# A planned instruction order with other prices for transfers and returns, and more PSUM banks at a phase's end and start

## The chip, the cores and the metric

The kernel runs on one core of a Trainium2 chip. TensorE (PE) multiplies matrices into the eight banks of PSUM; VectorE (DVE), ScalarE (ACT) and GpSimd (POOL) work on what lies in SBUF and PSUM; SyncE (SP) issues transfers (DMA). Each engine runs its instructions in the order in which they were written, and waits for others at semaphores. The metric is the time of one execution on the device, in microseconds (us).

## The reference, cut to what matters

It is one decoder layer in fp32, for a prompt of 1024 tokens and for eight single-token samples with a paged cache. All share their weights. A layer is a half-step feed-forward, a mixing step, and a second half-step feed-forward:

```python
h = x + 0.5 * rmsnorm(swiglu(rmsnorm(x, lp['n_ffn1_pre']), lp['ffn1_gate'], lp['ffn1_up'],
                             lp['ffn1_down']), lp['n_ffn1_post'])
u = rmsnorm(h, lp['n_mix_pre'])
proj = u @ lp['w_in']
q, k, v = jnp.split(proj[..., :3 * D_A], 3, axis=-1)
pb = proj[..., 3 * D_A:]
...
```

The columns of `proj` go to differential attention (4 heads; for the samples also over 512 cached tokens) and to an RWKV-7 recurrence (8 heads with a 64x64 state, run over the tokens). Both results are joined, multiplied by `w_out`, normalised and added to `h`; then the second feed-forward follows. The model is 1024 wide and the feed-forward 2816.

## The kernel before, in words

Activations lie transposed, 128 channels by tokens, and the tokens (prompt and samples) are cut into two halves of two chunks. The wide products keep fp32 accuracy by splitting each operand into a high and a low part and adding three products of a faster format ("split products"). Small products of the mixing are full fp32, one product each. When TensorE goes from those back to split products, this text calls it a return.

The trunk (`s_trunk`, L1031) has four phases, numbered 0 to 3 in the code, and called the first to the fourth in the prediction: the first feed-forward of half 0, that of half 1, the second feed-forward of half 0, that of half 1. Phases 0 and 3 multiply part of their blocks by a scheme with seven products in place of eight (`FAST`, `seven`); phases 1 and 2 (`WIDE`) work 512 columns wide. Each phase runs through groups of hidden blocks: gate and up products (operands `pre_X`, `pre_T` in the profile), then the down products of the group before (`trunk_xl`, and in places `trunk_dreg`). The last group's down products are called the tail here. Each tail product is evicted by VectorE into `trunk_xl`, and its squares are summed (`trunk_acc`). A stream `s_tail` then makes the norm: a product with ones (`tail_aux`; `last_aux` after phase 2), a square root on ScalarE, a reciprocal on VectorE, and a scaling of the eight blocks. During phase 1 the mixing of half 0 runs beside the wide products, during phase 2 that of half 1: projections (`proj`), four RWKV jobs a half (`job`), attention (`attn`), the output projection (`outb`), and the samples' attention over their pages (`dec_dreg`). An RWKV job brings data into another layout by a store to memory and a load back: eight times through `Md` and eight times through `Xd`.

PSUM's banks have names: m0 to m3, aux0, aux1, cb, dec. `ps()` (L246) hands a trunk product the next bank of the stream's list `banks`, which changes with the phase (L1047, L1228). Before the change phases 1, 2 and 3 open on m0 and m1 (phase 3 with aux1), and the tails of phases 1 and 2 stay on m0 and m1. `SIX` is the pair m2, m3. The four row transposes of a finished block (`rows_cb`) use the one bank cb, which a copy to `rows_X` empties.

Which engine does what, and in which order, is planned in the program. Every step of these streams is only recorded (`put`; all rows of the profile so bear one line, L325). `price` (L386) gives each a duration, and `run` (L484) then picks, again and again, the step that can start first over the five engines, within `SLACK` by its priority. For a transfer it adds up: 1.17 us from the issue to its start on the shared rings, the time on the rings, and `LAND` until it counts as seen. TensorE's steps cost more where they follow others of another kind: a return costs `MODE`. The planning is repeated `PASSES` times. Each repetition gives every step a latest start (`latest`), which orders the next one; the plan with the smallest planned end becomes the program. A price so changes the order of everything behind it, on all engines. Some steps (`either`, `choose`) also go to VectorE or to GpSimd by the plan, the subtraction that makes the low part of a weight (`wts_w`) among them.

## Time and profile before

| | |
|---|---|
| median of 3 runs | 2241.69 us (2241.63 to 2242.61) |
| the profiled execution | 2243.7 us, span 2241.9 us |
| mean granted TensorE clock | 0.994 |
| TensorE busy | 2187.3 us, 98% of the span |
| VectorE, ScalarE, GpSimd busy | 1559.9, 1085.1, 1007.8 us |
| moved by DMA | 338.84 MB, 151 GB/s on average |

The profile is of one execution on the chip. Rows of a time line give start, duration, engine, operation, result <- operands, shapes and count, and in brackets the idle time before and whom it waited for. Rows of a cut into windows give the length, each engine's busy time with its count of instructions, the granted clock of TensorE (1.00 is full), the busy share of the DMA engines and GB/s. The clock is granted in stretches of 3.41 us.

### The profile page before, as it was taken

To read this page: it belongs to the slowest core of one execution; us is meant where nothing else is said; L and a number is where in the kernel's file an instruction comes from. 1 tells how busy PE (TensorE), PEld (TensorE's weight loads), DVE (VectorE), ACT (ScalarE), POOL (GpSimd) and SP (SyncE) were. 2 spreads that over 40 slices of the span, in tenths; PEclk is the share of its full clock that TensorE was granted. 3 is DMA by queue.
4 is the path that set the end of the run, shared out by engine and by line. 5 is a ranking of instruction groups with operands and counts; after the bars stand their busy time and mean duration, and the time that the engine had idled before them with its cause. 6 is when DMAs were issued, how large, how long until landed. Compare 5 with 4: busy or idle time off the path is not lost. (4 is left out here: it accounts for less than half of the span.)

```text
span 2241.9 us, 42167 instructions
## 1 busy us (share of the span) xinstructions
PE 2187.3 (98%) x15551; PEld 1960.6 (87%) x15551; DVE 1559.9 (70%) x3608; ACT 1085.1 (48%) x2233; POOL 1007.8 (45%) x834
## 2 busy tenths in 40 slices
PE   8999999999999989999999999999999999999998
PEld 8999998899887778898887777778888989999998
DVE  7868887656667787647775667776765366777776
ACT  6434444644553347344454445435655455444444
POOL 4545555533333673456453332335443355444443
PEclk9999999999999999999999999999999999999999
DMA  7322233445343674755564534476337838342343
GB/s 262 111 95 87 94 113 124 132 149 140 100 116 103 190 213 132 218 156 164 164 205 156 145 115 129 136 221 199 114 103 220 275 115 290 118 151 99 138 147 108
DMA packets 216088, 338.84 MB, mean 151 GB/s; under 512 B 50731, under 2 KB 130379, under 8 KB 215883
## 3 DMA queue, kind: packets, MB, share of 16 engines
q1 hardware_dynamic: 215594, 335.63, 47.9%
q8 instruction: 123, 2.02, 0.4%
q14 instruction: 83, 0.67, 0.1%
q10 hardware_dynamic: 288, 0.52, 0.1%
HBM read 281.06 MB, written 55.03 MB: 150 GB/s over the span
## 5 line engine op out<-in xcount | busy, mean ns | idle before, releaser
L325 POOL TENSOR_TENSOR wts_w<-wts_raw,wts_w 128x1024 fp32r<-128x1024 f32 (+2 forms) x160 | 301.2, 1886 | 356.8 <-ACT wts_w L325 301.1
L325 PE MATMUL trunk_m<-trunk_xl,wts_w 128*128 128x256 f32 (+2 forms) x2574 | 421.7, 316 | 0.4 <-DVE trunk_xl L325 0.4
L325 PE MATMUL trunk_m<-pre_X,wts_w 128*128 128x512 f32 (+3 forms) x2040 | 390.0, 344 | 9.6 <-ACT wts_w L325 6.0
L325 PEld LDWEIGHTS trunk_m<-trunk_xl,wts_w 128*128 128x128 f32 x2574 | 359.3, 188 | 29.4 <-issue 1.6
L325 PE MATMUL trunk_m<-pre_T,wts_w 128*128 128x512 f32 (+3 forms) x1800 | 364.6, 353 | 6.7 <-DVE trunk_xl L325 6.6
L325 PEld LDWEIGHTS trunk_m<-pre_X,wts_w 128*128 128x128 f32 x2040 | 312.8, 190 | 51.7 <-ACT wts_w L325 6.0
L325 ACT CAST wts_w<-wts_raw 128x512 fp32r<-128x512 f32 (+3 forms) x299 | 242.3, 826 | 211.1 <-PE trunk_m L325 123.0
L325 PEld LDWEIGHTS trunk_m<-pre_T,wts_w 128*128 128x128 f32 x1800 | 285.1, 191 | 47.3 <-issue 4.9
L325 PE MATMUL proj_m<-tail_xl,lin_w 128*128 128x256 f32 (+2 forms) x1920 | 320.9, 322 | 0.5 <-DVE init_E L325 0.5
L325 PEld LDWEIGHTS proj_m<-tail_xl,lin_w 128*128 128x128 f32 x1920 | 270.7, 188 | 35.0 <-issue 9.6
L325 DVE TENSOR_TENSOR trunk_xl<-trunk_xl,trunk_m 128x256 f32<-128x256 f32 (+2 forms) x362 | 172.5, 490 | 53.1 <-PE trunk_m L325 52.2
L325 POOL TENSOR_TENSOR lin_w<-lin_raw,lin_w 128x1024 fp32r<-128x1024 f32 x41 | 99.7, 2432 | 221.4 <-ACT lin_w L325 211.4
L325 POOL TENSOR_TENSOR trunk_xl<-trunk_t,trunk_xl 128x260 fp32r<-128x260 f32 (+3 forms) x87 | 93.7, 1078 | 132.9 <-ACT trunk_xl L325 128.9
L325 DVE TENSOR_TENSOR wts_w<-wts_raw,wts_w 128x1024 fp32r<-128x1024 f32 (+3 forms) x109 | 114.1, 1052 | 13.9 <-ACT wts_w L325 13.5
L325 POOL TENSOR_TENSOR wts_w<-wts_lraw,wts_w 128x512 fp32r<-128x512 f32 x57 | 78.5, 1380 | 60.1 <-ACT wts_w L325 57.4
L325 ACT CAST lin_w<-lin_raw 128x1024 fp32r<-128x1024 f32 x52 | 54.5, 1047 | 74.6 <-PE proj_m L325 54.0
L325 PE MATMUL trunk_m<-comb_T,wts_w 128*128 128x260 f32 x660 | 84.7, 283 | 0.0
L325 PEld LDWEIGHTS trunk_m<-comb_T,wts_w 128*128 128x128 f32 x660 | 81.7, 188 | 0.0
L325 ACT CAST wts_w<-wts_lraw 128x512 fp32r<-128x512 f32 x100 | 58.7, 619 | 38.5 <-POOL wts_lraw L325 12.5
L325 PE MATMUL trunk_aux<-trunk_xl,wts_w 128*128 128x256 f32 (+1 forms) x546 | 75.1, 282 | 0.0
L325 ACT CAST trunk_xl<-trunk_t 128x512 fp32r<-128x512 f32 (+3 forms) x94 | 45.4, 484 | 50.4 <-DVE trunk_t L325 49.7
L325 PEld LDWEIGHTS trunk_aux<-trunk_xl,wts_w 128*128 128x128 f32 x546 | 69.5, 189 | 0.0
(614 smaller groups left out, 4088.0 us busy)
## 6 DMA issues: line engine op xcount, KB each, us to landing
wts_raw<-in_ffn_gate_dram SPq DMA_DIRECT2D x87, 512.0 KB
wts_raw<-in_ffn_up_dram SPq DMA_DIRECT2D x56, 512.0 KB
lin_raw<-in_w_in_dram SPq DMA_DIRECT2D x52, 512.0 KB
wts_raw<-in_ffn_down_dram SPq DMA_DIRECT2D x52, 384.0 KB
wts_raw<-in_ffn_down_dram SPq DMA_DIRECT2D x31, 512.0 KB
wts_w<-Ld SPq DMA_DIRECT2D x22, 512.0 KB
wts_lraw<-in_ffn_down_dram SPq DMA_DIRECT2D x18, 512.0 KB
mix_T<-out_dram SPq DMA_DIRECT2D x36, 256.0 KB
```

The lines of the kernel that those rows point to most:

```text
L325: o = Op(eng, lambda: fn(*a, **k), st)
```

## The change

Prices first. A load now counts as seen 1.6 us after its time on the rings, a store 0.6, where both took 2.0. Issuing a transfer on SyncE costs 0.44 with 128 partitions, 0.62 with fewer, 1.14 with runs of at most 64 bytes, where it was 0.47. A return costs 0.03 us and 0.00043 us for each column of the product before it (0.25 after 512 columns, 0.06 after 64), where it was 0.085. A ScalarE step that reads PSUM into fewer than 128 partitions with more than two dimensions costs 0.1 more. The plan is repeated ten times in place of eight. Then banks: phase 3 opens on five (m0 to m3, aux1) in place of three. The tails of phases 1 and 2 wait until the output projection of half 0 or of half 1 is done; behind that wait phase 2's tail uses four banks in place of two, and phase 1's still two.

```diff
@@ -93,7 +93,7 @@
 MW = 1
 MARG = 0
 SLACK = 0.02
-PASSES = 8
+PASSES = 10
 BIAS = {}
 SHIFT = {}
 MIX = 1
@@ -104,7 +104,7 @@
 LOWS = (1, "out")
 STARVE = 1
 STICK = 0
-MODE = 0.085
+MODE = 0.03
 HOLD = 0.6
 HUNGER = 0.1
 RB = "dec"
@@ -170,14 +170,15 @@
 
 
 TV = 0.2
-LAND = 2.0
+LAND = 1.6
+STORE = 0.6
 MPE = 0.0
 HOP = {"tensor": (0.0, TV, TV, 0.22, 0.2), "vector": (0.18, 0.127, 0.13, 0.155, 0.13), "scalar": (0.165, 0.14, 0.143, 0.165, 0.15),
        "gpsimd": (0.31, 0.08, 0.15, 0.12, 0.15), "sync": (0.2, 0.15, 0.15, 0.15, 0.0)}
 
 
 class Op:
-    __slots__ = ("eng", "call", "cost", "load", "columns", "dma", "left", "ready", "start", "end", "seen", "then", "st", "ins", "table", "deps", "tile", "port", "late", "key", "before")
+    __slots__ = ("eng", "call", "cost", "load", "columns", "dma", "loads", "wide", "left", "ready", "start", "end", "seen", "then", "st", "ins", "table", "deps", "tile", "port", "late", "key", "before")
 
     def __init__(self, eng, call, st):
         self.eng, self.call, self.st = eng, call, st
@@ -398,7 +399,9 @@
                     run *= d.pop()[1]
                 runs.append(4 * run)
             run = min(runs)
-            o.cost = 1.04 if o.eng == "gpsimd" else 1.4 if op == "page_dma" else 0.47
+            near = out if out.space != bass.MemoryType.DRAM else ins[0]
+            o.loads = near is out
+            o.cost = 1.04 if o.eng == "gpsimd" else 1.4 if op == "page_dma" else 1.14 if run <= 64 else 0.44 if near.shape[0] == P else 0.62
             o.dma = n * out.shape[0] * 4 / run * (9 + 0.041 * run) / 16e3
         elif o.eng == "tensor":
             m = a[1].shape[1]
@@ -414,7 +417,7 @@
             o.columns, o.load = f * n * a[1].shape[0] / P, m / 1600
             r, c = a[1].start_partition(), out.start_partition()
             o.tile = r, r + a[1].shape[0], c, c + out.shape[0], out.tensor.name
-            o.table = f == 1
+            o.table, o.wide = f == 1, n
         elif o.eng == "vector":
             two = (a[1], a[3]) if op == "scalar_tensor_tensor" else ins if op == "tensor_tensor" else [x for x in ins if tuple(x.shape[1:]) != (1,)]
             wide = [x for x in two if x.space != PSUM]
@@ -424,7 +427,7 @@
             o.cost = 0.07 + n / (160 if op == "reciprocal" else 480 if op == "tensor_tensor_scan" else 1920 if fast else 960) \
                 + (0.05 if op == "scalar_tensor_tensor" else 0.06 * scalars)
         elif o.eng == "scalar":
-            o.cost = (0.06 if ins[0].space == PSUM else 0.093) + n / 1195 + 0.093 * scalars + 0.093 * ("accum_out" in k)
+            o.cost = (0.093 if ins[0].space != PSUM else 0.16 if len(out.shape) > 2 and out.shape[0] < P else 0.06) + n / 1195 + 0.093 * scalars + 0.093 * ("accum_out" in k)
         else:
             o.port = True
             o.cost = (0.2 if op == "scalar_tensor_tensor" else 0.156 if op == "tensor_tensor" else 0.06) + n / (470 if op == "tensor_tensor" else 960)
@@ -486,7 +489,7 @@
         table, turn, round_ = "exp", None, True
         last = self.last = {}
         warm, tick, passed = True, 0, 4096.0
-        rings, tile, size, credit, paced = 0.0, None, None, 0.0, 0.0
+        rings, tile, size, credit, paced, width = 0.0, None, None, 0.0, 0.0, 0
         lanes = deque([0.0] * 8)
         while self.streams:
             n = None
@@ -534,8 +537,8 @@
                     s = max(s, free["tensor"] + 0.09)
                     o.cost += 0.04
                 if o.table and not round_:
-                    o.cost += MODE * (size == (t[1] - t[0], t[3] - t[2]))
-                round_ = o.table
+                    o.cost += (MODE + 0.00043 * width) * (size == (t[1] - t[0], t[3] - t[2]))
+                round_, width = o.table, o.wide
                 size = t[1] - t[0], t[3] - t[2]
                 if u is not None and s < free["tensor"] + 0.01 and (t[0] >= u[1] or u[0] >= t[1]) and (t[2] >= u[3] or u[2] >= t[3] or t[4] != u[4]):
                     o.cost, tile = 0.05 if t[1] - t[0] == 64 else 0.028, None
@@ -554,7 +557,7 @@
                 held[o.eng], turn = o.end, o.eng
             if o.dma:
                 rings = max(rings, s + (1.69 if o.eng == "gpsimd" else 1.17)) + o.dma
-                o.seen = rings + LAND
+                o.seen = rings + (LAND if o.loads else STORE)
                 if o.eng != "gpsimd":
                     lanes.append(o.seen + 0.1)
                     lanes.popleft()
@@ -1044,7 +1047,7 @@
                 ring = self.T(self.big, [P, 4160], "xl1", FR)
             wide = ph in WIDE
             few = ("m0", "m1")
-            self.cur.banks = few + {0: SIX, 3: ("aux1",)}.get(ph, ())
+            self.cur.banks = few + {0: SIX, 3: SIX + ("aux1",)}.get(ph, ())
             yc = []
             cut = lambda t, n: [self.parts(ph, t[:, 1040 * j:1040 * j + 520], t[:, 1040 * j + 520:1040 * j + 1040]) for j in range(n)]
             if ph == 2:
@@ -1227,6 +1230,9 @@
                             self.signal(f"lead{ph}")
             if ph in FAST:
                 self.cur.banks = few + (("aux1",) if ph else ("m2", "m3"))
+            else:
+                yield ("wait", ("outw", ph - 1))
+                self.cur.banks = few + SIX[:2 * (ph == 2)]
             yield from down(len(groups) - 1, True)
         self.signal("trunk")
```

The work itself is the same: both programs have 14171 steps on TensorE, and on the other engines the counts differ by three at most. The order differs almost everywhere. These are the places that matter below.

VectorE, at the end of phase 0 (`trunk_m` 128x264 are the evictions of the tail's second chunk, `tail_aux` the norm of the first). Before:

```order
L325 TENSOR_TENSOR trunk_xl_126_796<-trunk_xl_126_796,trunk_m_647_4941 128x264
L325 TENSOR_TENSOR trunk_acc_4799<-trunk_acc_4799,trunk_sq_4942 128x264
L325 TENSOR_TENSOR trunk_xl_126_796<-trunk_xl_126_796,trunk_m_651_4954 128x264
L325 TENSOR_TENSOR trunk_xl_126_796<-trunk_xl_126_796,trunk_m_653_4966 128x264
L325 RECIPROCAL tail_aux_641_4895<-trunk_acc_4798 128x256
L325 TENSOR_TENSOR trunk_acc_4799<-trunk_acc_4799,trunk_sq_4967 128x264
L325 TENSOR_TENSOR trunk_xl_126_796<-trunk_xl_126_796,trunk_m_655_4977 128x264
L325 TENSOR_TENSOR tail_aux_641_4895<-tail_aux_641_4895,init_rb_113 128x256
L325 SCALAR_TENSOR_TENSOR tail_T_639_4893<-trunk_xl_126_796,init_cols_96,tail_aux_641_4895 128x256
L325 TENSOR_TENSOR trunk_acc_4799<-trunk_acc_4799,trunk_sq_4978 128x264
L325 TENSOR_TENSOR trunk_xl_126_796<-trunk_xl_126_796,trunk_m_657_4989 128x264
```

And now:

```order
L326 TENSOR_TENSOR trunk_xl_126_796<-trunk_xl_126_796,trunk_m_647_4941 128x264
L326 TENSOR_TENSOR trunk_acc_4800<-trunk_acc_4800,trunk_sq_4942 128x264
L326 TENSOR_TENSOR trunk_xl_126_796<-trunk_xl_126_796,trunk_m_651_4955 128x264
L326 TENSOR_TENSOR trunk_xl_126_796<-trunk_xl_126_796,trunk_m_653_4966 128x264
L326 TENSOR_TENSOR trunk_xl_126_796<-trunk_xl_126_796,trunk_m_655_4977 128x264
L326 TENSOR_TENSOR trunk_xl_126_796<-trunk_xl_126_796,trunk_m_657_4989 128x264
L326 RECIPROCAL tail_aux_641_4895<-trunk_acc_4799 128x256
L326 TENSOR_TENSOR tail_aux_641_4895<-tail_aux_641_4895,init_rb_113 128x256
L326 SCALAR_TENSOR_TENSOR tail_T_639_4893<-trunk_xl_126_796,init_cols_96,tail_aux_641_4895 128x256 x4
L326 SCALAR_TENSOR_TENSOR tail_T_640_4894<-trunk_xl_126_796,init_cols_96,tail_aux_641_4895 128x256
L326 TENSOR_TENSOR trunk_acc_4800<-trunk_acc_4800,init_rb_113 128x264
```

The last two evictions stood behind the reciprocal; now all eight stand ahead of it, and the sums of squares come later.

VectorE, at the end of phase 2 (`last_aux` is the norm, `rows_X` the copy that empties cb). Before:

```order
L325 TENSOR_TENSOR trunk_xl_1740_14927<-trunk_xl_1740_14927,trunk_m_2372_20056 128x256
L325 TENSOR_TENSOR trunk_acc_19831<-trunk_acc_19831,trunk_sq_20063 128x256
L325 TENSOR_TENSOR trunk_xl_1740_14927<-trunk_xl_1740_14927,trunk_m_2374_20076 128x256
L325 TENSOR_TENSOR trunk_xl_1740_14927<-trunk_xl_1740_14927,trunk_m_2378_20093 128x256
L325 RECIPROCAL last_aux_2367_20040<-trunk_acc_19830 128x256
L325 TENSOR_TENSOR trunk_acc_19831<-trunk_acc_19831,trunk_sq_20106 128x256
L325 TENSOR_TENSOR trunk_xl_1740_14927<-trunk_xl_1740_14927,trunk_m_2380_20115 128x256
L325 SCALAR_TENSOR_TENSOR trunk_xl_1740_14927<-trunk_xl_1740_14927,init_cols_96,last_aux_2367_20040 128x256 x5
```

And now:

```order
L326 TENSOR_TENSOR trunk_xl_1741_14929<-trunk_xl_1741_14929,trunk_m_2372_20056 128x256
L326 TENSOR_TENSOR trunk_xl_1741_14929<-trunk_xl_1741_14929,trunk_m_2374_20074 128x256
L326 TENSOR_TENSOR trunk_xl_1741_14929<-trunk_xl_1741_14929,trunk_m_2378_20093 128x256
L326 TENSOR_TENSOR trunk_xl_1741_14929<-trunk_xl_1741_14929,trunk_m_2380_20115 128x256
L326 COPY rows_X_2327_19811<-rows_cb_19818 128x512
L326 RECIPROCAL last_aux_2367_20038<-trunk_acc_19839 128x256
L326 TENSOR_TENSOR trunk_acc_19840<-trunk_acc_19840,trunk_sq_20123 128x256
L326 SCALAR_TENSOR_TENSOR trunk_xl_1741_14929<-trunk_xl_1741_14929,init_cols_96,last_aux_2367_20038 128x256 x8
```

The last eviction stood behind the reciprocal; now it stands ahead of it, and so does a copy of `rows_cb`, which TensorE's transposes there need.

TensorE, at the same place, where phase 3 begins with `pre_T`. Before:

```order
L325 MATMUL trunk_m_2378_20093<-trunk_xl_1780_15296,wts_w_2357_19968 128x256 x6
L325 MATMUL last_aux_2367_20040<-trunk_acc_19830,init_onesD_76 128x256
L325 MATMUL trunk_m_2378_20093<-trunk_xl_1780_15296,wts_w_2357_19968 128x256 x3
L325 MATMUL trunk_m_2380_20115<-trunk_xl_1780_15296,wts_w_2357_19968 128x256 x9
L325 MATMUL rows_cb_19815<-init_ident_69,outb_T_2177_18395 128x128 x4
L325 MATMUL trunk_m_2393_20146<-pre_T_2282_19371,wts_w_2376_20084 128x264
L325 MATMUL trunk_m_2393_20146<-pre_T_2283_19372,wts_w_2376_20084 128x264
L325 MATMUL trunk_m_2393_20146<-pre_T_2282_19371,wts_w_2376_20084 128x264 x2
```

And now:

```order
L326 MATMUL trunk_m_2378_20093<-trunk_xl_1766_15161,wts_w_2357_19968 128x256 x9
L326 MATMUL trunk_m_2380_20115<-trunk_xl_1766_15161,wts_w_2357_19968 128x256 x9
L326 MATMUL rows_cb_19818<-init_ident_69,outb_T_2176_18395 128x128 x4
L326 MATMUL last_aux_2367_20038<-trunk_acc_19839,init_onesD_76 128x256
L326 MATMUL trunk_m_2393_20142<-pre_T_2278_19338,wts_w_2376_20085 128x264
L326 MATMUL trunk_m_2393_20142<-pre_T_2279_19339,wts_w_2376_20085 128x264
L326 MATMUL rows_cb_19819<-init_ident_69,outb_T_2177_18396 128x128 x4
L326 MATMUL trunk_m_2393_20142<-pre_T_2278_19338,wts_w_2376_20085 128x264 x2
L326 MATMUL trunk_m_2393_20142<-pre_T_2279_19339,wts_w_2376_20085 128x264
```

The norm's product `last_aux` moved behind the tail, and the second set of four transposes behind two products of phase 3. By the lists of banks, the first `pre_T` product had to take one of three banks, of which the tail had just used two; now it is one of five, and the tail uses four.

VectorE, in the attention of half 0 (`mix_T<-attn_m` scales what TensorE's next small products multiply; `dec_dreg` is the samples' attention). Before:

```order
L325 TENSOR_REDUCE dec_dreg_8752<-dec_dreg_8752 128x4x2
L325 TENSOR_SCALAR mix_T_1073_9225<-attn_m_1085_9237,attn_sm_1080_9232 128x128
L325 TENSOR_REDUCE attn_mx_1087_9239<-attn_aux_1088_9240 128x1
L325 TENSOR_REDUCE dec_dreg_8752<-dec_dreg_8752 128x4x2
L325 TENSOR_REDUCE attn_mx_1087_9239<-attn_m_1089_9241 128x1
L325 TENSOR_REDUCE dec_dreg_8752<-dec_dreg_8752 128x4x2
L325 TENSOR_TENSOR trunk_t_9656<-trunk_g_9655,trunk_m_1160_9682 128x512
L325 RECIPROCAL attn_sm_1086_9238<-attn_sm_1086_9238 128x2
L325 SCALAR_TENSOR_TENSOR attn_sm_1086_9238<-attn_sm_1086_9238,aset_nlam_141 128x1
L325 SCALAR_TENSOR_TENSOR mix_w_1072_9224<-mix_w_1072_9224,attn_sm_1086_9238 128x384
L325 TENSOR_SCALAR mix_T_1073_9225<-attn_m_1108_9260,attn_sm_1103_9255 128x128
```

And now:

```order
L326 TENSOR_SCALAR mix_T_1062_9099<-attn_m_1074_9111,attn_sm_1069_9106 128x128
L326 SCALAR_TENSOR_TENSOR mix_w_1061_9098<-mix_w_1061_9098,attn_sm_1092_9129 128x256
L326 TENSOR_REDUCE attn_mx_1076_9113<-attn_aux_1077_9114 128x1
L326 TENSOR_TENSOR mix_X_1064_9101<-mix_T_1063_9100,mix_X_1064_9101 64x512
L326 TENSOR_REDUCE attn_mx_1076_9113<-attn_m_1078_9115 128x1
L326 TENSOR_TENSOR wts_w_1150_9536<-wts_raw_9481,wts_w_1150_9536 128x1024
L326 TENSOR_REDUCE dec_dreg_8794<-dec_dreg_8794 128x4x2
L326 RECIPROCAL attn_sm_1075_9112<-attn_sm_1075_9112 128x2
L326 SCALAR_TENSOR_TENSOR attn_sm_1075_9112<-attn_sm_1075_9112,aset_nlam_141 128x1
L326 TENSOR_REDUCE dec_dreg_8794<-dec_dreg_8794 128x4x2
L326 TENSOR_SCALAR mix_T_1062_9099<-attn_m_1097_9134,attn_sm_1092_9129 128x128
L326 TENSOR_REDUCE attn_mx_1099_9136<-attn_aux_1100_9137 128x1
```

Reductions of `dec_dreg` still stand ahead of such scalings, but not of the same ones, and other small steps stand between.

## The prediction

> **What bounds the kernel now.** I read the page's table of engines first, then TensorE's waits, then the span cut into stages, and last the time lines at the places where the stages lose time.
>
> ```profile
> PE 2187.3 (98%) x15551; PEld 1960.6 (87%) x15551; DVE 1559.9 (70%) x3608; ACT 1085.1 (48%) x2233; POOL 1007.8 (45%) x834
> ...
> PE trunk_m L325 <- DVE trunk_xl L325: 8.0, 5, 3.8
> PE attn_m L325 <- DVE mix_T L325: 6.3, 4, 2.6
> PE job_aux L325 <- DVE job_hres L325: 4.9, 3, 3.0
> PE tail_aux L325 <- DVE trunk_acc L325: 1.1, 1, 1.1
> ```
>
> TensorE is busy for 2187.3 of 2241.9 us, so it is the bound, and a new order can win only the other 54.6 us and what TensorE loses while it counts as busy. The wait rows (total, times, longest) say for whom it idles. The opening and the last instructions stand in the same order in both kernels, so their waits are left at nothing. The stages show where the rest lies (columns: the length, each engine's busy time and count, the granted clock, DMA).
>
> ```profile
> 374.00:388.00 14.00, 9.38 (x30) 7.20 (x31) 10.87 (x22) 3.65 (x7) 7.86 (x11) 0.76 0.22 75
> 490.00:900.00 410.00, 396.35 (x2998) 334.36 (x2997) 288.61 (x812) 199.59 (x470) 183.25 (x131) 0.99 0.49 142
> 1200.00:1560.00 360.00, 347.39 (x2337) 274.31 (x2337) 251.39 (x666) 165.37 (x333) 140.29 (x84) 1.00 0.54 155
> 1815.00:1880.00 65.00, 60.76 (x421) 56.59 (x420) 39.93 (x72) 35.00 (x62) 33.29 (x42) 0.97 0.60 195
> ```
>
> The switch from the first to the second phase (374 to 388) idles 4.6 us and has a clock of 0.76. The two mixing stages, in which small products stand among the wide ones, idle 13.7 and 12.6 us. The switch from the third to the fourth phase idles 4.2 us. So the change has two switches and the mixing to act on.
>
> **The switch from the first to the second phase.**
>
> ```profile
> 375.46 1.00 PE L325 MATMUL trunk_m<-trunk_xl,wts_w 128*128 128x264 f32 x6
> 380.31 7.96 PE L325 MATMUL trunk_m<-pre_T,wts_w 128*128 128x512 f32 x22 [3.85 <-DVE trunk_xl L325]
> ...
> 376.31 0.76 DVE L325 TENSOR_TENSOR trunk_xl<-trunk_xl,trunk_m 128x264 f32<-128x264 f32 x2
> 377.74 1.76 DVE L325 RECIPROCAL tail_aux<-trunk_acc 128x256 f32<-128x256 f32 x1 [0.67 <-ACT trunk_acc L325]
> 379.75 0.42 DVE L325 TENSOR_TENSOR trunk_xl<-trunk_xl,trunk_m 128x264 f32<-128x264 f32 x1
> ```
>
> TensorE finishes the first phase's last product at 376.46 and starts the second phase's first at 380.31, because that product's PSUM bank is emptied by the eviction of 379.75, which stands on VectorE behind a reciprocal (0.67 us of waiting, then 1.76). In the changed order all eight 264-column evictions stand ahead of the reciprocal. The seventh then follows the pair that ends at 377.07. Two evictions there take 0.76 us, so it ends by about 377.42, and TensorE starts 0.14 us later (380.31 less the 380.17 at which the old eviction ends): 377.56, a gain of 2.75 us. What is late next is the chain of that reciprocal: the tail's normalised rows come some 0.7 us later relative to the evictions. They feed the projections tens of microseconds later, and the next product on that chain stands behind some 33 products of the new phase, so I cost it at nothing. Without that cover it costs the 0.7.
>
> The second part is the clock. The rows give the length of a window, the busy time of TensorE in it, and the granted clock.
>
> ```profile
> 375.78:379.20 3.42, 0.68 (x6) 1.00 0.21 84
> 379.20:386.02 6.82, 5.71 (x14) 0.50 0.01 3
> 737.60:741.01 3.41, 1.40 (x14) 1.00 0.51 111
> 741.01:747.84 6.83, 6.83 (x39) 0.50 0.61 188
> 812.69:816.10 3.41, 1.94 (x11) 1.00 1.03 339
> 816.10:819.52 3.42, 2.52 (x13) 1.00 0.98 242
> 1464.63:1468.05 3.42, 0.84 (x32) 1.00 0.55 149
> 1468.05:1471.46 3.41, 3.41 (x13) 0.50 1.00 304
> 1867.41:1870.82 3.41, 0.72 (x6) 1.00 0.98 368
> 1870.82:1874.24 3.42, 3.42 (x18) 0.50 1.02 380
> ...
> 1804.56 16.86 PE L325 MATMUL trunk_m<-trunk_xl,wts_w 128*128 128x512 f32 x72
> ```
>
> The clock falls to a half behind the windows with at most 1.40 us of work (375.78, 737.60, 1464.63, 1867.41), and stays full behind the one with 1.94. At the full clock one 512-column product takes 16.86/72 = 0.234 us, so the 22 at 380.31 would take 5.15 us and took 7.96: 2.81 us lost. With the restart at 377.56 the window holds 0.68 + 1.64 = 2.32 us of work, above 1.94. Another execution may cut its windows elsewhere. The worst cut spans the neighbouring 1.1 us wait of `tail_aux` too and leaves about 1.6, between the two bounds; I take the full clock, and keep the half clock for the upper end. Sum: 2.75 + 2.81 = **-5.55 us**; bounds -2.4 (the bank waits for the eighth eviction as well, and the half clock stays) and -5.6.
>
> [...]
>
> **The switch from the third to the fourth phase.**
>
> ```profile
> 1866.74 0.60 PE L325 MATMUL rows_cb<-init_ident,outb_T 128*128 128x128 f32 x4
> 1870.10 6.13 PE L325 MATMUL trunk_m<-pre_T,wts_w 128*128 128x264 f32 x36 [2.77 <-DVE trunk_xl L325]
> ...
> 1859.61 0.69 DVE L325 COPY rows_X<-rows_cb 128x512 f32<-128x512 f32 x1
> ...
> 1867.56 1.76 DVE L325 RECIPROCAL last_aux<-trunk_acc 128x256 f32<-128x256 f32 x1 [1.27 <-ACT trunk_acc L325]
> 1869.55 0.41 DVE L325 TENSOR_TENSOR trunk_xl<-trunk_xl,trunk_m 128x256 f32<-128x256 f32 x1
> ```
>
> It is the same picture: the bank of the fourth phase's first product is emptied at 1869.55, behind a reciprocal that itself waits 1.27 us. With four banks in the third phase's tail and five in the fourth's opening, that product gets a bank that has long been empty, and all evictions stand ahead of the reciprocal besides. This removes 2.77 us. The window at 1867.41 (0.72 us of work) then holds about 3 us, so the half clock of the window after it goes as well: it did in 3.42 us what takes 1.71, so 1.71 us. Something is added: four transposes of `rows_cb` now stand behind two products of the new phase and wait for the copy that empties the one `cb` bank. That copy (0.69) follows the last eviction (0.41); the four transposes, one `last_aux` product and two products ahead cover about 0.8 us, so TensorE waits 0.3 to 0.6 us, and I take 0.4. If the copy fell behind the reciprocal it would be up to 1.8, the half clock would still be avoided. Sum: -2.77 - 1.71 + 0.4 = **-4.1 us**; bounds -1.0 (half clock kept, the whole 1.8) and -4.5.
>
> **A weight and the returns.**
>
> ```profile
> 1823.34 3.50 PE L325 MATMUL trunk_m<-pre_X,wts_w 128*128 128x512 f32 x14 [1.45 <-POOL wts_w L325]
> ...
> 1820.91 2.37 POOL L325 TENSOR_TENSOR wts_w<-wts_raw,wts_w 128x1024 fp32r<-128x1024 f32 x1 [1.94 <-ACT wts_w L325]
> ...
> L325 DVE TENSOR_TENSOR wts_w<-wts_raw,wts_w 128x1024 fp32r<-128x1024 f32 x50 | 64.5, 1290 | 10.6 <-ACT wts_w L325 10.5
> ```
>
> The subtraction that the product of 1823.34 waits for moves from GpSimd (2.37 us) to VectorE (1.29 on average): 1.1 us less of a 1.45 us wait, if VectorE is free at once; part of that it will not be. I take **-0.7 us**; bounds 0 and -1.45. Returns from full-precision small products to the split wide ones fall from 388 to 380, since the plan now prices them by the width of the product before. No row of the trace prices a return alone; the nearest is the 0.234 us of one split product. If a return loses nothing, or just such a product, eight are worth 0 or 1.9 us, and I take **-0.7**, a little under the middle.
>
> **The mixing stages.** The other prices act here. Loads from memory are now taken to land 0.4 us sooner, stores 1.4 us sooner, and the issue of short-run transfers costs more of the queue's time. The work is the same. What changes is where the small products stand among the wide ones: for half 0 some 5 to 14 us of TensorE work earlier, for half 1 a few us later up to about 1500 and then alike. Two kinds of stall matter.
>
> ```profile
> 817.00 0.44 PE L325 MATMUL attn_m<-mix_X 128*128 128x384 f32 x1 [2.37 <-DVE mix_T L325]
> ...
> 816.00 0.69 DVE L325 TENSOR_REDUCE dec_dreg<-dec_dreg 128x8 f32<-128x512 f32 x1 [3.43 <-POOL dec_dreg L325]
> ...
> 1419.07 1.65 DMA Md<-job_w
> ...
> 1422.79 3.24 DMA job_lraw<-Md
> ...
> 1455.75 5.02 DMA Xd<-job_hres
> 1460.85 5.55 DMA bset_TT<-Xd
> ...
> 1466.98 0.24 PE L325 MATMUL job_aux<-job_hres,job_w 32*32 32x32 f32 x2 [3.01 <-DVE job_hres L325]
> ```
>
> The attention's products wait for a scaling that stands on VectorE behind a reduction of the decode stream, which waits 3.43 us for its own input. In the changed order reductions of the decode stream still stand ahead of such scalings, with other steps between, so these stalls move rather than go. The second kind is the round trip through memory: 10.6 us for one `Xd` store and load together, and TensorE stalls 3.01. An undisturbed store and load (1.65 + 3.24 = 4.9) is near the new plan: the 1.77 and 2.77 us that it takes from issue are 4.5 together, where the old was 6.3 (3.17 twice). So the new prices fit the quiet case, and leave 1.8 us less room in the loaded one. I expect the 26.3 us of idle time in the two stages to be drawn afresh, with somewhat less room: **+1.5 us**. The bounds are wide, since every stall is a coincidence of streams: -7 (the two stalls named here, 2.37 and 3.01, go with one half clock of 1.7) and +8 (four to five round trips lose the 1.8).
>
> The second phase's tail gets a new wait, for the end of half 0's output projection, and keeps its two banks. In the order nothing shows that it is held up, so it costs nothing, under cover of a projection that ends well ahead. Without that cover the price is one late transfer of the decode stream, some 3.4 us like the 3.43 above, since pages are issued later there.
>
> **Sum.** -5.55 - 4.1 - 0.7 - 0.7 + 1.5 = -9.55. The profiled execution took 2243.7 us (1.8 more than its span), so 2234.2 for one like it. The median of the runs is 2.0 below that execution, so **2232 us**.
>
> **The rivals.** Rival 1, the mixing eats it, on the other side. Round trips and pages are planned to land earlier than they do in a loaded queue, and TensorE, which works strictly in order, stands. The kernel makes 16 round trips (32 stores each of `Md` and `Xd` in the order, four to a trip). At 1.8 us each on eight of them, and one half clock of 1.7 us for every third stall, it loses 14.4 + 4.5 = 19 against the 11.05 that the other terms win: +8, so 2250. It decides from five exposed round trips on (11.05 over 1.8 and a third of 1.7). For it speaks the 10.6 us trip, against it that three waits for `job_hres`, 4.9 us in all, are what TensorE shows of them today. Rival 2, the gains are given back to within 0.2%: the half clock at the first switch stays (2.81) and the mixing loses 5 us: -11.05 + 2.81 + 5 = -3.2, so 2238.5. Rival 3, something other than these stalls halves the clock, and it stays half behind both switches: -9.55 + 2.81 + 1.71 = -5.0, so 2236.7. The four windows speak against it. [...] Rival 4, the mixing gains: the stalls at 817.00 and 1466.98 vanish with a half clock, -5.4 - 1.7 in place of the +1.5: 2223.5.
>
> **How the numbers follow.** About 0.2% (4.5 us) is what a measurement of this kernel can tell from no change. Forecast 0.46, rival 1 0.13, rival 2 0.17, rival 3 0.08, rival 4 0.16. The likeliest case alone runs from 2227 to 2237 by the bounds of its terms. Leaving out rival 1 and the far edge of rival 4, the range is 2223 to 2243. Faster takes the forecast, rival 4, half of rival 3 and a little of rival 2: 0.70. Slower takes most of rival 1: 0.10. No change is the rest, 0.20.
>
> **What would show it.** In the changed profile the gap ahead of the second phase's first `pre_T` product is about 1.1 us (from 3.85), with no half clock behind it; the fourth phase's first `pre_T` product starts with no wait for `trunk_xl`; a wait of `rows_cb` for `rows_X` of under half a microsecond stands there; and idle time in 490 to 900 and 1200 to 1560 stays at 20 to 34 us in all. The forecast is wrong if that sum passes 36 us, or if a half clock follows either switch.

## The result, and the profile after

The changed kernel takes 2255.8 us (median of 5 runs, 2253.51 to 2259.98), the kernel before 2241.63 us (median of 5). The ratio is 1.0064, with a 95% interval of 1.0052 to 1.0076: 14 us slower. The profiled execution has a span of 2253.6 us, 11.7 more than the one of before. The sign of the prediction was wrong. A profile is of one execution, and executions of one kernel lie up to ten us apart (2236.4 to 2246.8 us in 14 runs of the kernel before on one chip), so a difference of 2 or 3 us between two profiles is no more than a hint.

TensorE's row of the page, and the first rows of its waits (total, times, longest), in the changed kernel:

```profile
PE 2192.9 (97%) x15551; PEld 1960.3 (87%) x15551; DVE 1565.2 (69%) x3611; ACT 1085.9 (48%) x2230; POOL 1016.3 (45%) x836
...
PE job_aux L326 <- DVE job_hres L326: 6.5, 5, 3.8
...
PE job_aux L326 <- DVE mix_X L326: 3.8, 4, 2.5
PE trunk_m L326 <- DVE trunk_xl L326: 3.7, 7, 1.1
PE decf_dec L326 <- DVE dec_dreg L326: 3.5, 1, 3.5
PE attn_aux L326 <- ACT mix_X L326: 3.3, 1, 3.3
```

The wait for `trunk_xl`, on which both switches rested, fell from 8.0 to 3.7 us. In its place stand waits for what the mixing's transfers feed. The span cut at the first product of each phase shows where the time went. First the kernel before, from its first product on, one row for a phase (length, TensorE's busy time, granted clock, DMA share, GB/s):

```profile
6.00:380.31 374.31, 367.78 (x3025) 1.00 0.38 127
380.31:1116.51 736.20, 721.10 (x4964) 0.99 0.50 151
1116.51:1870.10 753.59, 735.73 (x4568) 1.00 0.55 166
```

And the changed kernel:

```profile
5.66:379.39 373.73, 369.01 (x3024) 1.00 0.39 127
379.39:1128.60 749.21, 724.42 (x4963) 0.99 0.50 148
1128.60:1881.08 752.48, 737.00 (x4564) 1.00 0.54 165
```

The second phase, with the mixing of half 0, became 13.0 us longer. Its idle time rose from 15.1 to 24.8 us. The third phase ends 1.1 us shorter, since it won 4 us at its end and lost 3 in the mixing of half 1.

**The first switch.** TensorE's products, two windows of the clock, and VectorE, in the changed kernel:

```profile
377.30 0.99 PE L326 MATMUL trunk_m<-trunk_xl,wts_w 128*128 128x264 f32 x6
379.39 7.88 PE L326 MATMUL trunk_m<-pre_T,wts_w 128*128 128x512 f32 x33 [1.10 <-DVE trunk_xl L326]
...
375.60:379.02 3.42, 2.06 (x12) 1.00 0.45 145
379.02:382.43 3.41, 3.04 (x13) 1.00 0.02 8
...
368.60 0.42 DVE L326 TENSOR_TENSOR trunk_acc<-trunk_acc,trunk_sq 128x256 f32<-128x256 f32 x1 [2.58 <-POOL trunk_acc L326]
...
378.15 1.44 DVE L326 TENSOR_TENSOR trunk_xl<-trunk_xl,trunk_m 128x264 f32<-128x264 f32 x4
379.58 1.76 DVE L326 RECIPROCAL tail_aux<-trunk_acc 128x256 f32<-128x256 f32 x1
```

The gap is the 1.10 us that was forecast, and no half clock follows: 33 products took 7.88 us, 0.239 each. But TensorE reaches the last six products of the tail 1.8 us later than before (377.30 against 375.46). VectorE stood 2.58 us at a sum of squares that waits for GpSimd, with the evictions behind it.

**The third switch**, from the third to the fourth phase (phase 3 in the code). TensorE, and VectorE's copy:

```profile
1880.84 0.60 PE L326 MATMUL last_aux<-trunk_acc,init_onesD 128*128 128x256 f32 x2
1881.08 0.59 PE L326 MATMUL trunk_m<-pre_T,wts_w 128*128 128x264 f32 x2
1881.78 0.65 PE L326 MATMUL rows_cb<-init_ident,outb_T 128*128 128x128 f32 x4
1882.19 2.08 PE L326 MATMUL trunk_m<-pre_T,wts_w 128*128 128x264 f32 x15
...
1881.04 0.69 DVE L326 COPY rows_X<-rows_cb 128x512 f32<-128x512 f32 x1
```

The first `pre_T` product waits for nothing, where it had waited 2.77 us, and the transposes behind it wait for the end of the copy. From 1881.08 to 1881.78 stand two products, at 0.14 us each by the row of 15, so 0.4 us are lost, as forecast.

**One wait of the mixing, followed back.** The queue of SyncE, GpSimd, VectorE, TensorE, and then two windows of the clock, in the changed kernel:

```profile
733.64 0.34 SPq L326 DMA_DIRECT2D Qd<-dec_dreg  x1
...
737.91 0.37 SPq L326 DMA_DIRECT2D dec_dreg<-Qd  x1
...
743.31 3.71 POOL L326 TENSOR_TENSOR dec_dreg<-dec_dreg 128x512 f32<-128x512 f32 x3 [10.03 <-DMA dec_dreg<-Qd]
...
744.60 0.69 DVE L326 TENSOR_REDUCE dec_dreg<-dec_dreg 128x8 f32<-128x512 f32 x1 [5.54 <-POOL dec_dreg L326]
...
746.48 0.36 PE L326 MATMUL decf_dec<-dec_dreg,bset_wa 64*128 64x8 f32 x2 [3.51 <-DVE dec_dreg L326]
...
744.00:747.00 3.00, 0.52 (x4) 1.00 1.01 235
747.00:753.83 6.83, 6.83 (x25) 0.50 0.68 209
```

A store of 32 rows to `Qd` is issued at 733.64. The load that reads it back can be issued only at 737.91, 4.3 us later, and its reader on GpSimd starts at 743.3, 5.4 us after that. The new prices say 1.77 and 2.77 us from the issue, and the time on the rings; the plan has 1.83 us for this store and 3.73 for this load. On VectorE the reduction that waits for this stands ahead of an unrelated eviction (`trunk_g`), the state update and the steps that feed TensorE. TensorE idles 3.51 us, the 3.00 us ahead of the half clock hold 0.52 us of its work, and 6.8 us at half clock follow: 3.4 us more. The next long wait also stands behind late transfers. ScalarE, VectorE and TensorE:

```profile
803.47 0.62 ACT L326 CAST mix_X<-mix_T 128x512 fp32r<-128x512 f32 x1 [4.31 <-DMA mix_T<-out_dram]
...
804.59 0.17 DVE L326 RECIPROCAL attn_sm<-attn_sm 128x2 f32<-128x2 f32 x1 [4.46 <-ACT mix_w L326]
...
805.15 0.44 PE L326 MATMUL attn_aux<-init_ident,mix_w 128*128 128x128 f32 x1 [3.26 <-ACT mix_X L326]
```

A cast on ScalarE waits 4.31 us for a load from `out_dram`. The four loads of `mix_T` that were issued just before (794.91 to 798.75) landed after 5.4 to 8.1 us, and the plan has 3.2 to 4.0. Behind it in ScalarE's order stands the exponential for the other attention unit, for which VectorE waits 4.46 and TensorE 3.26 us, although its own data was there.

### The profile page after: what moved, and what is told of

Its sections match the earlier page's. It is cut to its first block, busy times and chain, and to the rows that moved or that the text cites. A ratio compares the mean times of both kernels' runs of the same rounds, so it can differ in the third digit from the quotient of the medians.

```text
span 2253.6 us, 42135 instructions
## 1 busy us (share of the span) xinstructions
PE 2192.9 (97%) x15551; PEld 1960.3 (87%) x15551; DVE 1565.2 (69%) x3611; ACT 1085.9 (48%) x2230; POOL 1016.3 (45%) x836
## 5 line engine op out<-in xcount | busy, mean ns | idle before, releaser
L326 POOL TENSOR_TENSOR wts_w<-wts_raw,wts_w 128x1024 fp32r<-128x1024 f32 (+2 forms) x168 | 319.2, 1903 | 349.4 <-ACT wts_w L326 287.7
L326 DVE TENSOR_TENSOR wts_w<-wts_raw,wts_w 128x1024 fp32r<-128x1024 f32 (+3 forms) x101 | 103.3, 1027 | 12.9 <-ACT wts_w L326 11.5
L326 POOL TENSOR_TENSOR wts_w<-wts_lraw,wts_w 128x512 fp32r<-128x512 f32 x52 | 70.7, 1361 | 51.2 <-ACT wts_w L326 50.0
L326 ACT CAST wts_w<-wts_lraw 128x512 fp32r<-128x512 f32 x100 | 58.7, 619 | 39.8 <-DMA wts_lraw<-in_ffn_down_dram 12.3
L326 ACT CAST wts_w<-wts_dec 128x512 fp32r<-128x512 f32 x32 | 18.8, 588 | 104.6 <-DVE wts_dec L326 93.6
```

The lines of the kernel that those rows point to most:

```text
L326: o = Op(eng, lambda: fn(*a, **k), st)
```

## The experiments

All runs of a kernel below are compared with runs of the kernel before on the same chip, whose median there lies between 2239.0 and 2241.1 us. With each stands the end that the program's own plan has (`predicted` in `run`). That is no measurement. It is what the planner believes under its prices, and the measured median less that end is called the slip here: by how much the execution falls behind the plan. The kernel before plans 2225.1 us and slips by 14 to 17; the changed one plans 2220.2 and slips by 35.6.

The plan has a start for every step, so the trunk's products, which stand in one sequence in plan and profile, say where a profiled execution falls behind. The first phase keeps to the plan (the changed kernel ends it 0.6 us ahead, the kernel before 1.1), and the fourth nearly so (1.0 and 2.5 us behind). In the second phase the changed kernel falls 20.4 us behind and the kernel before 4.9, in the third 9.3 and 7.3. So the slip arises in the mixing.

The ten repetitions in place of eight need no run. In the kernel before the best of ten plans is the same as of eight, and in the changed kernel the best is the sixth, so that number changes neither. Of the runs below that plan ten times, only "longer landings" ends on one of the last two plans, 0.2 us ahead of the best of the first eight.

**Old banks.**

```diff
-            self.cur.banks = few + {0: SIX, 3: SIX + ("aux1",)}.get(ph, ())
+            self.cur.banks = few + {0: SIX, 3: ("aux1",)}.get(ph, ())
...
-            else:
-                yield ("wait", ("outw", ph - 1))
-                self.cur.banks = few + SIX[:2 * (ph == 2)]
```

> The changed kernel with only its bank lists put back (phase 3 opens on three banks, the tails of phases 1 and 2 on m0 and m1, no wait for the output projection); all new prices stay. Its order is the same as the changed kernel's on TensorE up to the end of phase 2 and differs only behind it. Theory 'banks pay, prices cost': the gain at the third switch, about 4.1 us, is the banks' alone, so this kernel takes 2260 (2258 to 2262) where the changed one takes 2255.8, the wait of 2.8 us ahead of phase 3 is back with a half clock behind it, and everything ahead of phase 2's tail stays as late as in the changed kernel. Rival 'the prices made that gain too': no wait ahead of phase 3, 2256 (2254 to 2258).

Measured: 2254.27 us, ratio 1.0058 (1.0041 to 1.0075). The rival held: the prices made that gain too. TensorE at the third switch of this kernel:

```profile
1882.52 3.73 PE L326 MATMUL trunk_m<-pre_T,wts_w 128*128 128x264 f32 x26 [0.39 <-DVE trunk_xl L326]
```

Only 0.39 us of the old 2.77 is back. With the evictions ordered ahead of the reciprocal, the bank is free nearly in time, with three banks as with five.

**Banks alone** (the same lines, added to the kernel before).

> The kernel before with only the new bank lists; all prices old. Theory 'banks pay, prices cost': it wins the third switch's 4 us and nothing else, 2237.5 (2235 to 2240), and the idle time of TensorE in the mixing of both halves stays near 26 us. Rival 'every new plan draws the mixing afresh': the order of the mixing changes with the banks too, since the plan is repeated with other latest starts, so it lands anywhere from 2230 to 2250, with the difference lying between 490 and 1560 us and not at the switch.

Measured: 2237.02 us, ratio 0.9990 (0.9981 to 1.0000). That is 2 us, at the edge of what can be told, and less than the 4 us of the switch. Its profiled execution has the gain at the switch (no wait ahead of phase 3, 0.42 us at the transposes), so in the profiles the banks pay where the old order stands, and either cause is enough for that gain. The mixing of half 0 is 3 us shorter in the profile as well, which the medians do not bear out.

**Old landings** (the changed kernel with `LAND = 2.0` and `STORE = 2.0`).

> The changed kernel with loads and stores both taken to land after 2.0 us again; other prices and banks new. Theory 'landings': the loss in the mixing of half 0, 11 us, comes from steps put too close behind round trips through memory (a rope block through out_dram, Qd, Md and Xd), so this kernel gets it back: 2244 (2241 to 2248), and TensorE's waits behind such trips (3.5 us for dec_dreg, 3.3 for mix_X, 2.5 for mix_X) are gone. Rival 'returns': the loss comes from the price of returns; 2256 (2252 to 2260) with such waits still there. Rival 'drawn afresh': 2240 to 2262 with waits of other names.

Measured: 2253.76 us, ratio 1.0052 (1.0035 to 1.0070). By what was expected the theory of the landings fell here. But this program's plan is another kind of bad: its own end is 2238.7 us, and the slip is 15.1, as in the kernel before. Much of its loss is one stretch of clock. Two rows of windows in this kernel:

```profile
722.70:726.12 3.42, 3.42 (x42) 1.00 0.26 98
726.12:746.60 20.48, 20.48 (x92) 0.50 0.41 113
```

TensorE is busy all the time in both, and the clock stays halved for 20.48 us, which is 10 us lost. So this run alone does not decide about the landings.

**Old returns** (the changed kernel with a return at 0.085 us).

> The changed kernel with a return priced at 0.085 us again, whatever the width before it; other prices and banks new. Theory 'landings': the loss stays, 2256 (2251 to 2260), and the longest waits of TensorE in the mixing are again behind transfers. Rival 'returns': the loss goes, 2243 (2240 to 2247). Rival 'drawn afresh': 2240 to 2262, with waits of other names.

Measured: 2251.50 us, ratio 1.0045 (1.0028 to 1.0062). The loss stays. The plan ends at 2222.9, the slip is 28.6.

So neither price, put back, gave the loss back. The next four runs went the other way and put single prices into the kernel before.

**Landings alone.**

```diff
-LAND = 2.0
+LAND = 1.6
+STORE = 0.6
...
-                o.seen = rings + LAND
+                o.seen = rings + (LAND if o.loads else STORE)
```

> The kernel before with only the new landings (loads 1.6 us, stores 0.6). Theory 'landings': the small products of half 0 stand earlier on TensorE (the attention's first at 638 us of wide work in place of 654) and wait behind trips through memory; the second phase takes 8 to 12 us longer than before, 2248 to 2254 in all. Theory 'drawn afresh': the second phase's length has nothing to do with this price; 2232 to 2256.

Measured: 2281.33 us, ratio 1.0182 (1.0165 to 1.0199): 42 us slower, far more than any theory had. Two phases of this kernel, cut as above, two stretches of its clock, and its longest waits:

```profile
379.61:1134.83 755.22, 732.94 (x4963) 0.97 0.49 147
1134.83:1915.10 780.27, 754.84 (x4568) 0.98 0.52 159
...
739.79:753.44 13.65, 13.65 (x57) 0.50 0.68 165
1320.05:1333.70 13.65, 13.65 (x91) 0.50 0.19 52
...
PE job_aux L326 <- DVE job_hres L326: 10.1, 7, 4.6
...
PE attn_aux L326 <- DVE mix_w L326: 5.7, 2, 4.8
```

`job_hres` is made by VectorE from what an `Xd` load brings. Beside the waits, TensorE's busy time in these two phases is 31 us more than in the kernel before (732.94 + 754.84 against 721.10 + 735.73), with the same instructions: that is half clock, 78.5 us of it in these phases against 15.9. The profiled execution was the slowest of four, 2287.9 us. The first of the two stretches shown does not follow a long wait: in the 3.41 us ahead of it (from 736.38) TensorE was busy for 2.99, with 30 mostly small products. So waits are only a part of it. The plan expected half clock for 17 us in its whole span, so the rest belongs to the slip. Why that window fills with small products was not followed.

**Returns alone** (the new price of a return in the kernel before).

> The kernel before with only the new price of a return (0.03 us and 0.00043 us a column of the product before). Theory 'landings': as fast as before or a little faster, 2236 to 2242. Theory 'returns': 2246 to 2256, the second phase 8 to 12 us longer. Theory 'drawn afresh': 2232 to 2256, and the sum of the three single prices' changes is far from the 15 us of all together.

Measured: 2236.78 us, ratio 0.9978 (0.9963 to 0.9993). A little faster. The plan ends at 2223.8, the slip is 13.0.

**Issue alone.**

```diff
-            o.cost = 1.04 if o.eng == "gpsimd" else 1.4 if op == "page_dma" else 0.47
+            near = out if out.space != bass.MemoryType.DRAM else ins[0]
+            o.cost = 1.04 if o.eng == "gpsimd" else 1.4 if op == "page_dma" else 1.14 if run <= 64 else 0.44 if near.shape[0] == P else 0.62
```

> The kernel before with only the new prices of issuing a transfer (0.44, 0.62 or 1.14 us in place of 0.47). Theory 'landings': as before, 2236 to 2242. Theory 'issue': since the old landings and the old returns each left the loss in place, what they share carries it, 2246 to 2256. Theory 'drawn afresh': 2232 to 2256.

Measured: 2229.71 us, ratio 0.9954 (0.9937 to 0.9970): 10 us faster, the best of all kernels here. The plan ends at 2224.3, hardly below that of the kernel before, and the slip is 5.4. The first three phases of this kernel:

```profile
5.82:380.70 374.88, 370.09 (x3024) 1.00 0.38 127
380.70:1116.08 735.38, 720.28 (x4963) 0.99 0.50 151
1116.08:1862.56 746.48, 735.74 (x4568) 1.00 0.54 167
```

In the profiles the gain is in the third phase, 7.1 us: TensorE's busy time there is that of the kernel before (735.74 against 735.73), and the idle time fell from 17.9 to 10.7. The profiled execution took 2234.7 us, the slowest of four.

**Another slack** (the kernel before with `SLACK = 0.03` in place of 0.02).

> The kernel before with all its prices and banks, and only SLACK 0.03 us in place of 0.02 (steps that can start within that of the earliest are chosen among by priority): a number that says nothing of transfers or returns. Its order is drawn afresh, with the attention of half 0 beginning at 643 us of wide work in place of 654, as early as in the changed kernel (648). Theory 'landings' or any one price: no systematic loss, 2234 to 2243. Theory 'drawn afresh': a difference as large as the change's own may appear, 2245 to 2256 if the early attention is what costs, with the loss between 640 and 850 us.

Measured: 2236.01 us, ratio 0.9985 (0.9976 to 0.9995). A new draw of the whole order, with the early attention, moves the time by 4 us and does not lose. So the early attention by itself does not make a loss of the change's size, and a new draw need not. The plan ends at 2223.7, the slip is 12.3.

**Loads alone, stores alone** (one of the two landings, in the kernel before).

> The kernel before with loads taken to land after 1.6 us in place of 2.0; stores stay at 2.0. Theory 'stores': the loss of the two landings together (42 us) is the store's, whose price fell by 1.4 us; this kernel is within 6 us of before, 2234 to 2246, with no long stretch of half clock. Rival 'loads': the 0.4 us counts at every weight and page, and steps stand too close behind all of them; 2255 to 2285.

> The kernel before with stores taken to land after 0.6 us in place of 2.0; loads stay at 2.0. Theory 'stores': most of the 42 us, 2260 to 2285, with TensorE's waits behind trips through memory (Xd, Md, Qd, the blocks of rope through out_dram) and long stretches of half clock. Rival 'loads': within 6 us of before, 2234 to 2246.

Measured: 2257.54 us, ratio 1.0085 (1.0065 to 1.0104), for the loads, and 2256.93 us, ratio 1.0078 (1.0060 to 1.0096), for the stores. Each theory had one of them near the kernel before; both fell. 0.4 us off every load costs as much as 1.4 us off every store, about 16 us each. The slips are 32.3 and 32.7.

**Old landings with another slack** (the run "old landings" again, with `SLACK = 0.03`).

> The changed kernel with the old landings, as in the run 'old landings', and SLACK 0.03 us in place of 0.02. There the loss of 14 us stayed though the landings were put back. Theory 'two things': a plan has its own end, which each new plan draws afresh (2238.7 us in that run's program, 2225.1 in the kernel before), and the execution slips behind it by 5 to 15 us with the old landings and by 29 to 49 with the new; this kernel's plan ends at 2227.0, so it takes 2232 to 2242. Rival 'another of the new prices costs too, with the banks or the step on ScalarE': 2248 to 2256 again.

Measured: 2237.32 us, ratio 0.9996 (0.9976 to 1.0015). The theory of two things held: with the old landings all the other parts of the change together are no slower than the kernel before, once the plan itself is drawn better. The plan ends at 2227.0, the slip is 10.3. This kernel differs from the changed one in two numbers, the landings and the slack. The changed kernel with the new slack alone was not run; in the kernel before that slack was worth 4 us of the 18 that lie between the two kernels here.

**Issue and banks** (both in the kernel before, the rest old).

> The kernel before with the new prices of issuing, the new banks, and ten repetitions of the plan; landings, returns and the ScalarE price are old. Theory 'two things': its plan ends at 2225.1, near that of the issue price alone (2224.3, measured 2229.7), so 2230 to 2238; the wait ahead of phase 3 is gone. Rival 'gains add up': 2229.7 less the 4 us of the banks at the third switch, 2224 to 2228. It beats both kernels by either.

Measured: 2232.27 us, ratio 0.9966 (0.9950 to 0.9982). It beats both kernels. The gains do not add up: it is no faster than the issue price alone.

**Old issue prices** (the changed kernel with 0.47 us for an issue).

> The changed kernel with issuing a transfer priced at 0.47 us again; landings, returns, the ScalarE price and the banks new. The landings alone cost 42 us, the whole change 15. Theory 'the issue price holds part of it': without it the execution slips behind its plan as with the landings alone, by 49 us or nearly so; the plan ends at 2216.7, so 2258 to 2270. Rival 'drawn afresh': the 42 was one bad draw and the slip of the changed kernel, 35 us, stays; 2248 to 2256.

Measured: 2266.68 us, ratio 1.0115 (1.0091 to 1.0139). As the theory had it: without the issue price the slip is 50.0, as with the landings alone (49.2). The plan is the most promising of all, with its end at 2216.7.

**Longer landings** (issue and banks, with `LAND = 2.4` and `STORE = 2.4`).

> The kernel before with the new prices of issuing and the new banks, as in the run 'issue and banks', and loads and stores taken to land after 2.4 us, longer than before. Theory 'the slip goes with the landing': the plan ends at 2231.8 and the execution slips by 0 to 6 us, 2232 to 2238; TensorE's waits behind transfers get rarer, and what is lost is in the plan itself. Rival 'the slip of 5 to 15 us has other causes': 2238 to 2247.

Measured: 2238.90 us, ratio 0.9999 (0.9985 to 1.0012), just outside the theory's range and inside the rival's. The plan that was built ends at 2231.6, so the slip is 7.3, that of the same kernel with 2.0 us (7.2), and the plan's end is 6.5 us later. In this draw the longer price only lengthens the plan.

All runs by their slip:

| kernel | load, store | issue | plan's end | measured | slip |
|---|---|---|---|---|---|
| issue alone | 2.0, 2.0 | new | 2224.3 | 2229.7 | 5.4 |
| longer landings, issue, banks | 2.4, 2.4 | new | 2231.6 | 2238.9 | 7.3 |
| issue and banks | 2.0, 2.0 | new | 2225.1 | 2232.3 | 7.2 |
| old landings, other slack | 2.0, 2.0 | new | 2227.0 | 2237.3 | 10.3 |
| other slack | 2.0, 2.0 | old | 2223.7 | 2236.0 | 12.3 |
| returns alone | 2.0, 2.0 | old | 2223.8 | 2236.8 | 13.0 |
| banks alone | 2.0, 2.0 | old | 2222.5 | 2237.0 | 14.5 |
| old landings | 2.0, 2.0 | new | 2238.7 | 2253.8 | 15.1 |
| before | 2.0, 2.0 | old | 2225.1 | 2239.0 to 2241.6 | 13.9 to 16.5 |
| old returns | 1.6, 0.6 | new | 2222.9 | 2251.5 | 28.6 |
| loads alone | 1.6, 2.0 | old | 2225.2 | 2257.5 | 32.3 |
| stores alone | 2.0, 0.6 | old | 2224.2 | 2256.9 | 32.7 |
| old banks | 1.6, 0.6 | new | 2220.7 | 2254.3 | 33.6 |
| changed kernel | 1.6, 0.6 | new | 2220.2 | 2255.8 | 35.6 |
| landings alone | 1.6, 0.6 | old | 2232.1 | 2281.3 | 49.2 |
| old issue | 1.6, 0.6 | old | 2216.7 | 2266.7 | 50.0 |

Every kernel with the old or longer landings slips by 5 to 17 us, every kernel with a shortened one by 29 to 50. With both landings short the new issue price takes 14 us off (50.0 to 35.6), alone 9 to 11. The plan's own end scatters from 2216.7 to 2238.7 and does not say which kernel is fast. A shorter price also makes a plan's end earlier by itself, but that is little of it: the mean end is 2223.1 with a shortened landing and 2226.9 without.

The plan also has a landing for every transfer, and the traces tell the real one for 1067 of 1088. Counted from the issue, 27% of them landed later than planned in the kernel before and 46% in the changed one. Over all runs it is 13 to 27% with the old or longer landings, 33% with loads or stores shortened, and 39 to 46% with both. In the changed kernel the median load took 4.1 us where 4.2 were planned, the median store 2.5 where 2.5 were planned.

## Why the prediction was wrong, point by point

**The first switch** was right in its mechanism and both its prices: the gap is 1.10 us, and the half clock is gone. Forecast were -5.55 us, measured about -3.4: the second phase starts 0.92 us earlier, 0.34 of it from the opening, and the half clock's 2.81 are saved. The missing 2.2 were lost ahead of the place that was looked at: three waits of TensorE between 369 and 373, behind VectorE's 2.58 us for a sum on GpSimd. The order of the evictions there had changed too, and only those around the reciprocal had been counted.

**The third switch** was right: -4.1 forecast, -4.4 measured over the 270 trunk products around it (41.4 to 37.0 us). Such stages are cut by counting the trunk's products, which stand in one sequence in both kernels. The reason was too narrow. The prediction gave the gain to the empty bank, with the order as an "all evictions stand ahead of the reciprocal besides". The run with old banks shows that this order alone removes 2.4 of the 2.8 us of waiting at the first product. Over the same 270 products that kernel takes 39.0 us, so the banks have the other half of the gain.

**The weight and the returns**: the stage with the weight of 1823.34 is as long as before (123.0 against 122.6 us), so the 0.7 us forecast for it did not show in the sum. The returns by their price alone are 3 us to the good, in a new draw of the order; what eight returns cost was not measured.

**The switch from the second to the third phase** was costed at nothing and lost about 4 us: idle time rose by 1.5 us, and a half clock followed that cost 1.7 us (granted 0.50 from 1119.06 to 1122.47). A weight's cast stands there on ScalarE behind a square that waits 0.86 us for an eviction (1116.21). The last 120 trunk products of the phase take 20.6 us, where they took 16.5, and 2.2 of these 4.1 stand already in the plan. The kernel with the issue price alone lost 3.4 us there too and the one with the landings alone nothing (16.5), so it is not the landings'. Nor is it the tail's new wait, which the prediction put at nothing: "old banks" lacks that wait and takes 20.6 us as well. Its cause is not settled.

**The mixing stages** are the step that failed: +1.5 us forecast, with bounds of -7 and +8. Measured are about +11.5 in half 0 and +3 in half 1, 14.5 together and outside the bounds. The failing sentence is "So the new prices fit the quiet case, and leave 1.8 us less room in the loaded one", with the idle time then "drawn afresh, with somewhat less room". It compared prices with one quiet trip through memory, 1.65 and 3.24 us, and took the loaded one (5.02 and 5.55) as the exception. It is no exception: the new prices are about the median, so that nearly half of the transfers came later than planned (46%). Each landing that does so can stop an engine at one instruction, and that engine holds all that stands behind it, for other streams as well, as in the two waits followed above (3.51 and 3.26 us on TensorE). The 1.8 us that the old prices were longer was the room that took this up. The run with loads alone shows how small the error may be: 0.4 us a load cost 16 us.

The prediction's own signs did not catch this. All that it named came true: the gap of 1.1 us, no half clock behind either switch, no wait at the fourth phase's first product, 0.4 us at the transposes. Idle time in 490 to 900 and 1200 to 1560 is 32.7 us in all (20.5 and 12.3), within its 20 to 34, while over the whole second phase it rose by 9.7.

**The rivals.** Rival 1 had the mechanism, the sign and the order of size: +8 forecast, +14 measured. Its place was too narrow. The waits that were followed back here lead to `Qd` and to the loads from `out_dram`, and loads cost as much as stores, where the prediction spoke of eight exposed trips through `Md` and `Xd`. In the changed kernel 35% of the transfers through `Md` and `Xd` landed later than planned, and 47% of the others; TensorE's waits for `job_hres`, which follow `Xd` loads, grew only from 4.9 to 6.5 us. At 0.13 its chance was too small. The prediction had held against it that few trips show on TensorE in the kernel before. That was weak evidence: under the old prices the median store landed 1.1 us ahead of its plan, so there was room for a late one. Rival 3 fell, since the half clocks at both switches went with their stalls. Rivals 2 and 4 did not happen.

**What stayed open.** That a shortened landing makes the execution slip is shown by the seven runs with one against the nine without. That it does so through steps behind late transfers is shown in the changed kernel for its 3.5 and 3.3 us waits, and the share of late transfers goes the same way in every run. How much of each loss is such a wait, and how much the half clock among small products, was not taken apart for the runs with one price. Why the issue price takes off slip, whether since SyncE's queue really is that slow or since it spaces the transfers out, was not tried apart either.

## What to carry to other kernels

A planner's price for a latency is a reserve as well as an estimate. Set to a quiet or a median value, as here, it placed consumers so tightly that 46% of the changed kernel's transfers landed later than planned, and engines stood behind them. So compare planned and executed positions over the whole span, and take a price that leaves the execution near its plan, not one that shortens the plan. A still longer one (2.4 us) won nothing more here. When prices that move everything are changed together, put each into the old kernel alone: here one part won 10 us and another lost 42, and only the sum was to be seen.

## What the runs showed of the hardware

In the run "old landings" a window in which TensorE was busy for 3.42 of 3.42 us, with 42 products, most of them 8 to 128 columns wide, was followed by 20.48 us at half clock, through which TensorE was busy all the time with small products among a few wide ones. In "landings alone" the window from 736.38 was busy for 2.99 of 3.41 us with 30 products and was followed by 13.65 us at half clock. So the windows that the prediction went by, with at most 1.40 us of work, are not the only ones in these runs with a half clock behind them. What decides it is not shown here.

A store of 32 rows to memory kept its reader from being issued for 4.3 us with the DMA engines 0.55 busy from 730 to 737 us (`Qd` at 733.64), where a quiet store of another kind (`Md`, in the kernel before) took 1.65. The reader of the load behind it started 5.4 us after that load's issue; the quiet load (`Md`) landed after 3.24.
